# A decoder step on one Trainium2 core: two attention blocks per head as one product of whole float32 operands

## The chip, the core and the metric

The kernel runs on one core of one Trainium2 chip. A core has five engines with a queue of instructions each: TensorE (matrix products, PE in the profile, with its weight loads as PEld), VectorE (DVE), ScalarE (ACT), GpSimd (POOL) and SyncE (SP), which here issues nearly all DMAs. TensorE reads both operands from the on-chip memory SBUF and writes its results to the accumulator memory PSUM. Engines wait for each other on semaphores.

The metric is the device time of one execution in microseconds (us), as a median over several executions. The kernel before takes 1631.18 us (median of 3, 1631.09 to 1631.23).

## What is computed

One layer of a decoder with three parallel branches (convolution, stick-breaking attention, attention into a memory), for a prompt of 256 tokens and 8 sampled sequences of 4 tokens. All of it is float32. The change lies in the stick-breaking attention of the prompt: 8 heads of 128 channels, strictly causal, in blocks of 128 queries.

```python
def stick_breaking_block(q, k, v, q_pos, k_pos, b_sb):
    z = jnp.einsum('bqhd,bkhd->bhqk', q, k).astype(jnp.float32) * (HEAD_DIM ** -0.5)
    z = z + b_sb.astype(jnp.float32)[None, :, None, None]
    causal = k_pos[None, :] < q_pos[:, None]
    log_keep = jnp.where(causal, jax.nn.log_sigmoid(-z), 0.0)
    after = lax.cumsum(log_keep, axis=3, reverse=True) - log_keep
    a = jnp.where(causal, jnp.exp(jax.nn.log_sigmoid(z) + after), 0.0)
    return jnp.einsum('bhqk,bkhd->bqhd', a.astype(v.dtype), v)
```

With 256 prompt tokens there are two blocks of queries. The first sees 128 keys, the second 256. So each head has three blocks of 128 x 128 scores: queries 0 to 127 against keys 0 to 127, and queries 128 to 255 against keys 0 to 127 and 128 to 255.

## The kernel before

**Split operands.** The kernel keeps float32 accuracy with products of a reduced type, `float32r`. An operand x is split into a high part h, its cast to that type on ScalarE, and a low part l = x - h, a subtraction on VectorE. A product of two split operands is three products: h by h, h by l and l by h, added up in PSUM. The weights are treated so on the way in: each slab of 128 x 1024 weights is loaded, cast (L303) and subtracted (L314). The large products over these slabs run at L486, with 128 stationary columns and 288 moving ones (256 prompt and 32 sample tokens).

**Order.** The order of all instructions is written out by a planner in the kernel (`Order`, L75). Each piece of work is a generator that asks for an engine with an estimated time, for flags that it needs and for buffers of the pools `a`, `t`, `s`, `k4`, `pm`, `pa`, `pl` and others; the planner always takes the request that can start first, by rank among equals. What comes out is one fixed queue for each engine. The main stream on TensorE is the large products, and the small ones of the attention heads are put between them.

**The heads.** For each of 8 heads the main stream makes a key, a query and a value tile (`sb_key`, `sb_query`, `sb_head`, started from L1420 to L1423). Key and query are normalised (`head_norm`) into a float32 tile `box[0]` and split (L1067, L1075) into a pair of tiles (`Pair`, L845). The value tile is transposed in two blocks (L1103, L1104) and split (L1108). Then `sb_head` computes

1. the scores: `three` (L849) at L1117 for the second 128 queries against all 256 keys, and at L1118 for the first 128 queries against the first 128 keys, both into one PSUM tile `zp` of 384 columns;
2. the attention weights from them on ScalarE and VectorE (L1122 to L1141);
3. three transposes (L1145), and the split of the 384 columns (L1148 on ScalarE, L1150 on VectorE);
4. the value product: `three` at L1157 with the first 128 values for all 256 queries, and at L1158 with the last 128 values for the last 128 queries, added to columns 128 to 255 of the same PSUM tile.

The helper `three` issues its products at L851, L852 and L853; all uses of it in the kernel, those of the memory attention too, show these lines. The product at L1225 (`first` in `sb_sample`, once for each of two groups of four sampled heads) is made of whole float32 operands, as are those of the sampled sequences at L1012, L1026 and L1182, which have 32 stationary columns.

Of the kernel before, what the change touches and what calls it, by code (L numbers as in the profile page):

```python
# [7 lines left out]
F32 = mybir.dt.float32  # L8
F32R = mybir.dt.float32r
# [5 lines left out]
P = 128  # L15
D_MODEL = 2048
KT = D_MODEL // P
NP = 256
# [3 lines left out]
T = NP + NS  # L22
# [52 lines left out]
class Order:  # L75
# [15 lines left out]
    def add(self, gen, rank, at=None):  # L91
        job = Job(gen, rank, self.now.ready if at is None and self.now else at or 0.0)
        self.jobs.append(job)
        was, self.now = self.now, job
        self.step(job)
        self.now = was
# [10 lines left out]
    def give(self, pool, n=1):  # L107
        self.pools[pool] += [self.now.ready] * n
# [45 lines left out]
def dve(n, *flags, **take):  # L154
    return Ask("DVE", 0.18 + n / 920.0, flags, **take)


def act(n, *flags, **take):
    return Ask("ACT", 0.22 + n / 1200.0, flags, **take)
# [6 lines left out]
def pe(us, *flags, **take):  # L166
    return Ask("PE", us, flags, **take)
# [15 lines left out]
def tile_decoder_step(ctx: ExitStack, tc: tile.TileContext, xT, memT, wall, cvec, kmat, ptab,  # L183
                      kpool, vpool, mkc, mvc, hist,
                      yT, oK, oV, oCp, oCs, oMK, oMV):
    nc = tc.nc
# [16 lines left out]
    give, add, done = order.give, order.add, order.set  # L203
# [3 lines left out]
    def tl(p, shape, dt=F32):  # L207
        cnt[0] += 1
        return pools[p].tile(shape, dt, tag=p, name=f"{p}_{cnt[0]}")

    def bank(p):
        return tl(p, [P, 512])
# [43 lines left out]
    def col(c):  # L256
        return cv[:, c:c + 1]
# [388 lines left out]
    def store(dst, src):  # L646
        yield sp(late=Order.HOP + Order.SLACK["SP"])
        nc.sync.dma_start(dst, src)
# [159 lines left out]
    def head_norm(ps, gcol, box, flag, p="pm"):  # L808

        yield dve(T, rx_done, t=4)  # L810
        raw, sq, hl, r = (tl("t", [P, T], F32R if i == 2 else F32) for i in range(4))
        nc.vector.tensor_mul(raw, ps, rx)
        give(p)
        yield act(T)
        nc.scalar.activation(sq, raw, AF.Square)
        yield dve(T)
        top, low = slice(0, P // 2), slice(P // 2, P)
        nc.vector.tensor_add(sq[top], sq[top], sq[low])
        yield act(T)
        nc.scalar.copy(hl[top], sq[top])  # L820
        yield dve(T)
        nc.vector.tensor_sub(hl[low], sq[top], hl[top].bitcast(F32))
        yield pe(MM, pa=1, late=1.5)
        ss = bank("pa")[:, :T]
        nc.tensor.matmul(ss, ones_r, hl, start=True, stop=True)  # L825
        yield from rsqrt_of(ss, T, HD, sq, r, r)
        give("pa")
        yield dve(T, a=1)
        out = tl("a", [P, T])
        nc.vector.scalar_tensor_tensor(out, raw, col(gcol), r, op0=ALU.mult, op1=ALU.mult)  # L830
        give("t", 4)
        box.append(out)
        done(flag)

    def split(a, src, n, flag=None):

        yield act(n, a=2)
        a.take()
        nc.scalar.copy(a.h[:, :n], src)
        yield dve(n)  # L840
        nc.vector.tensor_sub(a.l[:, :n], src, a.h[:, :n].bitcast(F32))
        if flag is not None:
            done(flag)

    class Pair:  # L845
        def take(self):
            self.h, self.l = tl("a", [P, T], F32R), tl("a", [P, T], F32R)

    def three(out, x, y, cx, cy, first=True, last=True):  # L849

        nc.tensor.matmul(out, x.h[:, cx], y.h[:, cy], start=first, stop=False)  # L851
        nc.tensor.matmul(out, x.h[:, cx], y.l[:, cy], start=False, stop=False)  # L852
        nc.tensor.matmul(out, x.l[:, cx], y.h[:, cy], start=False, stop=last)  # L853
# [201 lines left out]
    ks, qs_ = [None] * SH, [None] * SH  # L1055
    k_made, q_made, v_made = ([Flag() for _ in range(SH)] for _ in range(3))
# [3 lines left out]
    def sb_key(h):  # L1060
        def evac(ps):
            box, ks[h] = [], Pair()
            yield from head_norm(ps, C_GK, box, Flag())
            add(store(oK[h], box[0]), 3)
            yield act(NS)
            nc.scalar.copy(kn[:, h, :], box[0][:, NP:])
            yield from split(ks[h], box[0][:, :NP], NP, k_made[h])  # L1067
            give("a")
        return evac

    def sb_query(h):
        def evac(ps):
            box, qs_[h] = [], Pair()
            yield from head_norm(ps, C_GQ, box, Flag())
            yield from split(qs_[h], box[0][:, :NP], NP, q_made[h])  # L1075
            yield act(NS)
            nc.scalar.copy(qs[:, h, :], box[0][:, NP:])
            give("a")
            done(qs_made[h])
        return evac  # L1080

# [9 lines left out]
    def sb_head(h):  # L1091
        def evac(ps):
            yield dve(T, rx_done, a=1)
            v = tl("a", [P, T])
            nc.vector.tensor_mul(v, ps, rx)
            give("pm")
            add(store(oV[h], v), 3)
            yield act(NS)
            nc.scalar.copy(vs[:, h % 4 * NS:(h % 4 + 1) * NS], v[:, NP:])
            last = h % 4 == 3  # L1100
            yield pe(0.33 if last else 0.22, pa=1)
            tp = bank("pa")[:, :3 * P]
            nc.tensor.transpose(tp[:, 0:P], v[:, 0:P], ident)  # L1103
            nc.tensor.transpose(tp[:, P:2 * P], v[:, P:2 * P], ident)  # L1104
            if last:
                nc.tensor.transpose(tp[:, 2 * P:3 * P], vs, ident)
            vt = Pair()
            yield from split(vt, tp[:, :2 * P], 2 * P)  # L1108
            if last:
                yield act(P)  # L1110
                nc.scalar.copy(vn[:, h // 4, :], tp[:, 2 * P:3 * P])
            give("pa")
            give("a")
            done(v_made[h])
            yield pe(0.54, k_made[h], q_made[h], pa=1, s=3)
            zp = bank("pa")[:, :384]
            three(zp[:, 128:384], qs_[h], ks[h], slice(P, NP), slice(0, NP))  # L1117
            three(zp[:, 0:128], qs_[h], ks[h], slice(0, P), slice(0, P))  # L1118
            give("a", 4)
            z, l, sp_ = (tl("s", [P, 512]) for _ in range(3))  # L1120
            yield act(384)
            nc.scalar.activation(z[:, :384], zp, AF.Identity, scale=SCALE, bias=col(C_BSB + h))  # L1122
            give("pa")
            zz, ll, ss = z[:, :384], l[:, :384], sp_[:, :384]
            yield from softplus_parts(zz, ll)
            yield dve(384)
            nc.vector.scalar_tensor_tensor(ss, zz, 0.0, ll, op0=ALU.max, op1=ALU.add)
            yield dve(256)
            nc.vector.tensor_mul(blocks2(sp_, P), blocks2(sp_, P), twice(caus, P))
            yield dve(384)  # L1130
            nc.vector.scalar_tensor_tensor(zz, zz, 0.0, ll, op0=ALU.min, op1=ALU.subtract)
            yield dve(2 * 384)
            nc.vector.tensor_tensor_scan(ll[:, ::-1], ones_s[:, :384][:, ::-1], ss[:, ::-1], 0.0,
                                         op0=ALU.mult, op1=ALU.add)
            yield dve(384)
            nc.vector.tensor_sub(zz[:, :383], zz[:, :383], ll[:, 1:])
            give("s")
            yield act(384)
            act_fn(LN_EXP, zz, zz, AF.Exp)
            yield dve(256)  # L1140
            nc.vector.tensor_mul(blocks2(z, P), blocks2(z, P), twice(caus, P))  # L1141
            yield pe(0.35, pa=1)
            tp = bank("pa")[:, :384]
            for i in range(3):
                nc.tensor.transpose(tp[:, i * P:(i + 1) * P], z[:, i * P:(i + 1) * P], ident)  # L1145
            yield act(384, s=2)
            hh, low = tl("s", [P, 512], F32R), tl("s", [P, 512], F32R)[:, :384]
            nc.scalar.copy(hh[:, :384], tp)  # L1148
            yield dve(384)
            nc.vector.tensor_sub(low, tp, hh[:, :384].bitcast(F32))  # L1150
            give("pa")
            give("s", 2)
            w = Pair()
            w.h, w.l = hh, low
            yield pe(0.54, pa=1)
            op = bank("pa")[:, :NP]
            three(op, vt, w, slice(0, P), slice(0, NP), last=False)  # L1157
            three(op[:, P:NP], vt, w, slice(P, 2 * P), slice(256, 384), first=False)  # L1158
            give("s", 2)
            give("a", 2)  # L1160
            yield act(NP, a=2)
            a = osb[h] = Acts()
            nc.scalar.copy(a.h[:, :NP], op)
            yield dve(NP)
            nc.vector.tensor_sub(a.l[:, :NP], op, a.h[:, :NP].bitcast(F32))
            give("pa")
            done(osb_made[h])
        return evac
# [441 lines left out]
```

## Time and profile before

| what | before |
|---|---|
| median of 3 executions | 1631.18 us |
| profiled execution, its own time | 1630.64 us |
| its span, first to last instruction | 1628.9 us |
| granted clock of TensorE, mean | 1.000 |
| memory read, written | 296.99 MB, 6.32 MB |
| main products, L486, with pool `a` and high weights | x5184, 293 ns each |

The profile is one execution. "Busy" is the time in which an engine had an instruction running; an instruction's duration is a latency, and TensorE's instructions overlap, so what one costs is read from the distance between starts. A row of the groups gives line, engine, operation, output<-inputs, shapes, count, busy time and mean duration, and after the bar the idle time before it and what ended that. PEld rows are the weight loads of TensorE, which run beside its products. A row of the timeline merges equal neighbours and gives start, duration and count.

### The profile page before, as it was taken

To read this page: it belongs to the slowest core of one execution; us is meant where nothing else is said; L and a number is where in the kernel's file an instruction comes from. 1 tells how busy PE (TensorE), PEld (TensorE's weight loads), DVE (VectorE), ACT (ScalarE), POOL (GpSimd) and SP (SyncE) were. 2 spreads that over 40 slices of the span, in tenths; PEclk is the share of its full clock that TensorE was granted. 3 is DMA by queue.
4 is the path that set the end of the run, shared out by engine and by line. 5 is a ranking of instruction groups with operands and counts; after the bars stand their busy time and mean duration, and the time that the engine had idled before them with its cause. 6 is when DMAs were issued, how large, how long until landed. Compare 5 with 4: busy or idle time off the path is not lost.

```text
span 1628.9 us, 30880 instructions
## 1 busy us (share of the span) xinstructions
PE 1624.3 (100%) x12760; PEld 1608.8 (99%) x12760; DVE 996.7 (61%) x1478; ACT 737.9 (45%) x1066; POOL 139.0 (9%) x106
## 2 busy tenths in 40 slices
PE   9999999999999999999999999999999999999999
PEld 7999999999999999999999999999999999999999
DVE  7999888877777655565555544455445554455543
ACT  8846766654433534444443333333333333333332
POOL 0020000000000000001222200121001210022100
PEclk9999999999999999999999999999999999999999
DMA  9787474667755555556655555555555555555563
GB/s 327 226 182 256 151 263 150 223 224 275 282 179 169 167 170 170 168 160 207 195 172 168 171 173 168 167 171 172 168 169 168 168 169 168 169 168 169 180 193 100
DMA packets 107103, 305.33 MB, mean 187 GB/s; under 512 B 19922, under 2 KB 29522, under 8 KB 106962
## 3 DMA queue, kind: packets, MB, share of 16 engines
q1 hardware_dynamic: 106818, 303.33, 59.1%
q8 instruction: 100, 1.64, 0.4%
q14 instruction: 41, 0.34, 0.1%
q10 hardware_dynamic: 144, 0.02, 0.0%
HBM read 296.99 MB, written 6.32 MB: 186 GB/s over the span
## 4 chain that ended last, share of the span: by engine, by line
PE 100%; POOL 0%; DVE 0%; issue 0%; POOLq 0%
PE pm L486 93%; PE pm L539 3%; PE pa L486 1%; PE pl L1012 1%; PE pl L1182 0%; PE pa L853 0%; PE pa L852 0%; PE pa L851 0%; PE pl L1026 0%; PE pa L1406 0%; PE pa L825 0%; PE pa L1145 0%; PE pa L906 0%; PE pa L1103 0%; PE pa L633 0%; PE pa L1104 0%
## 5 line engine op out<-in xcount | busy, mean ns | idle before, releaser
L303 ACT CAST wh<-wr 128x1024 fp32r<-128x1024 f32 (+1 forms) x520 | 530.3, 1023 | 628.0 <-PE pm L486 568.7
L486 PE MATMUL pm<-a,wh 128*128 128x288 f32 x5184 | 739.1, 293 | 0.0
L314 DVE TENSOR_TENSOR wl<-wr,wh 128x1024 fp32r<-128x1024 f32 (+1 forms) x520 | 620.1, 1196 | 184.4 <-ACT wh L303 183.2
L486 PEld LDWEIGHTS pm<-a,wh 128*128 128x128 f32 x5184 | 695.9, 188 | 0.4 <-issue 0.4
L486 PE MATMUL pm<-a,wl 128*128 128x288 f32 x2592 | 397.9, 292 | 0.0
L486 PEld LDWEIGHTS pm<-a,wl 128*128 128x128 f32 x2592 | 358.3, 188 | 0.4 <-issue 0.4
L486 PE MATMUL pm<-k,wh 128*128 128x288 f32 x2400 | 337.9, 292 | 0.0
L486 PEld LDWEIGHTS pm<-k,wh 128*128 128x128 f32 x2400 | 321.0, 188 | 0.0
L486 PE MATMUL pm<-k,wl 128*128 128x288 f32 x1200 | 182.0, 292 | 0.0
L486 PEld LDWEIGHTS pm<-k,wl 128*128 128x128 f32 x1200 | 165.1, 188 | 0.0
L1343 POOL TENSOR_TENSOR t<-t 128x288 f32<-128x288 f32 x64 | 96.5, 1508 | 599.7 <-DVE t L1340 599.7
L1357 DVE TENSOR_TENSOR a<-a,pm 128x288 f32<-128x288 f32 x64 | 29.1, 455 | 122.7 <-PE pm L486 122.7
L1340 DVE SCALAR_TENSOR_TENSOR t<-pm,rx 128x288 f32<-128x288 f32 x64 | 29.2, 458 | 90.5 <-PE pm L486 90.5
L1346 ACT CAST k<-t 128x288 fp32r<-128x288 f32 x60 | 25.9, 433 | 123.9 <-POOL t L1343 123.9
L1259 DVE TENSOR_TENSOR t<-pm,rx 128x288 f32<-128x288 f32 x48 | 22.0, 458 | 76.2 <-PE pm L486 76.2
L1348 DVE TENSOR_TENSOR k<-t,k 128x288 fp32r<-128x288 f32 x60 | 27.4, 458 | 59.2 <-ACT k L1346 59.2
L717 DVE SCALAR_TENSOR_TENSOR a<-a,cv,a 128x256 f32<-128x256 f32 x120 | 59.5, 496 | 1.4
L1329 POOL TENSOR_TENSOR t<-t,t 128x288 f32<-128x288 f32 x15 | 21.3, 1418 | 389.9 <-ACT t L1326 389.9
L539 PE MATMUL pm<-wh,a 128*128 128x512 f32 x128 | 34.8, 394 | 0.0
L486 PE MATMUL pm<-s,wh 128*128 128x288 f32 x160 | 33.7, 292 | 0.0
L539 PEld LDWEIGHTS pm<-wh,a 128*128 128x128 f32 x128 | 24.3, 191 | 5.7 <-ACT wh L303 0.6
L486 PEld LDWEIGHTS pm<-s,wh 128*128 128x128 f32 x160 | 25.3, 188 | 0.0
(205 smaller groups left out, 755.3 us busy)
## 6 DMA issues: line engine op xcount, KB each, us to landing
wr<-in_wall SPq DMA_DIRECT2D x488, 512.0 KB, 3.6
wr<-in_wall SPq DMA_DIRECT2D x32, 256.0 KB, 4.9
k<-in_kpool SPq DMA_DIRECT2D x32, 256.0 KB, 5.9
k<-in_vpool SPq DMA_DIRECT2D x32, 256.0 KB, 6.1
k<-in_mkc SPq DMA_DIRECT2D x8, 512.0 KB, 8.6
k<-in_mvc SPq DMA_DIRECT2D x8, 512.0 KB, 7.2
t<-in_xT SPq DMA_DIRECT2D x16, 144.0 KB, 3.7
out_yT<-a SPq DMA_DIRECT2D x16, 144.0 KB, 1.9
```

What stands on the lines that cost most here:

```text
L303: nc.scalar.copy(sl.h[:, c], sl.raw[:, c])
L314: nc.vector.tensor_sub(sl.l[:, c], sl.raw[:, c], sl.h[:, c].bitcast(F32))
L486: nc.tensor.matmul(ps, w, a, start=(first and i == 0), stop=(last and i == len(todo) - 1))
L539: nc.tensor.matmul(ps[m], y[:, m * P:(m + 1) * P], z[:, w], start=(k == 0 and j < 2), stop=(k == KT - 1 and j in (4, 5)))
L717: nc.vector.scalar_tensor_tensor(c[:, :NP], up[:, k:k + NP], w, c[:, :NP], op0=ALU.mult, op1=ALU.add)
L1259: nc.vector.tensor_mul(g, ps, rx)
L1329: nc.gpsimd.tensor_add(sq_sum[0], sq_sum[0], res[0])
L1340: nc.vector.scalar_tensor_tensor(r, ps, 0.0, r2, op0=ALU.max, op1=ALU.mult)
L1343: nc.gpsimd.tensor_mul(r, r, r)
L1346: nc.scalar.copy(a.h, r)
L1348: nc.vector.tensor_sub(a.l, r, a.h.bitcast(F32))
L1357: nc.vector.tensor_add(x1[j], x1[j], ps)
```

## The change

The block of the first 128 queries against the first 128 keys, and the block of the last 128 attention weights against the last 128 values, are each one product of whole float32 operands. The parts that only these blocks used are no longer split: of the query, only the last 128 columns; of the value, only the first 128; of the transposed attention weights, only the first 256. The last block of values and of weights is copied from PSUM as it is, on ScalarE. The key is still split whole. A new class `Half` holds both parts in one tile.

```diff
     def split(a, src, n, flag=None):
-        yield act(n, a=2)
+        yield act(n, a=a.tiles)
...
     class Pair:
+        tiles = 2
         def take(self):
             self.h, self.l = tl("a", [P, T], F32R), tl("a", [P, T], F32R)
+    class Half:
+        tiles = 1
+        def take(self):
+            x = tl("a", [P, T], F32R)
+            self.h, self.l = x[:, :P], x[:, P:2 * P]
...
             nc.scalar.copy(kn[:, h, :], box[0][:, NP:])
+            ks[h].raw = box[0]
             yield from split(ks[h], box[0][:, :NP], NP, k_made[h])
-            give("a")
...
-            box, qs_[h] = [], Pair()
+            box, qs_[h] = [], Half()
             yield from head_norm(ps, C_GQ, box, Flag())
-            yield from split(qs_[h], box[0][:, :NP], NP, q_made[h])
+            qs_[h].raw = box[0]
+            yield from split(qs_[h], box[0][:, P:NP], P, q_made[h])
             yield act(NS)
             nc.scalar.copy(qs[:, h, :], box[0][:, NP:])
-            give("a")
...
-            vt = Pair()
-            yield from split(vt, tp[:, :2 * P], 2 * P)
+            vt = Half()
+            yield from split(vt, tp[:, :P], P)
+            yield act(P, a=1)
+            vt.raw = tl("a", [P, T])[:, :P]
+            nc.scalar.copy(vt.raw, tp[:, P:2 * P])
...
-            three(zp[:, 128:384], qs_[h], ks[h], slice(P, NP), slice(0, NP))
-            three(zp[:, 0:128], qs_[h], ks[h], slice(0, P), slice(0, P))
-            give("a", 4)
+            nc.tensor.matmul(zp[:, 0:128], qs_[h].raw[:, 0:P], ks[h].raw[:, 0:P], start=True, stop=True)
+            three(zp[:, 128:384], qs_[h], ks[h], slice(0, P), slice(0, NP))
+            give("a", 5)
...
-            yield act(384, s=2)
-            hh, low = tl("s", [P, 512], F32R), tl("s", [P, 512], F32R)[:, :384]
-            nc.scalar.copy(hh[:, :384], tp)
-            yield dve(384)
-            nc.vector.tensor_sub(low, tp, hh[:, :384].bitcast(F32))
+            yield act(256, s=2)
+            w, raw = Pair(), tl("s", [P, 512])
+            w.h, w.l = (lambda x: (x[:, :256], x[:, 256:]))(tl("s", [P, 512], F32R))
+            nc.scalar.copy(w.h, tp[:, :256])
+            yield act(P)
+            nc.scalar.copy(raw[:, :P], tp[:, 256:])
+            yield dve(256)
+            nc.vector.tensor_sub(w.l, tp[:, :256], w.h.bitcast(F32))
...
             three(op, vt, w, slice(0, P), slice(0, NP), last=False)
-            three(op[:, P:NP], vt, w, slice(P, 2 * P), slice(256, 384), first=False)
+            nc.tensor.matmul(op[:, P:NP], vt.raw, raw[:, :P], start=False, stop=True)
```

More of the change, by code (lines that the diff above doesn't have):

```diff
@@ L1145, in evac @@
                 nc.tensor.transpose(tp[:, i * P:(i + 1) * P], z[:, i * P:(i + 1) * P], ident)
-            yield act(384, s=2)
-            hh, low = tl("s", [P, 512], F32R), tl("s", [P, 512], F32R)[:, :384]
-            nc.scalar.copy(hh[:, :384], tp)
-            yield dve(384)
-            nc.vector.tensor_sub(low, tp, hh[:, :384].bitcast(F32))
+            yield act(256, s=2)
[6 more added lines that the diff above has]
+            nc.vector.tensor_sub(w.l, tp[:, :256], w.h.bitcast(F32))
             give("pa")
             give("s", 2)
-            w = Pair()
-            w.h, w.l = hh, low
             yield pe(0.54, pa=1)
```

## The prediction

> **What bounds the kernel now.** I read four views in this order: the first and fourth part of the page, the list of TensorE's waits, the table of stretches for the time in which the changed heads run, and then the timeline of single instructions around the products that change. First the page.
>
> ```profile
> span 1628.9 us, 30880 instructions
> ## 1 busy us (share of the span) xinstructions
> PE 1624.3 (100%) x12760; PEld 1608.8 (99%) x12760; DVE 996.7 (61%) x1478; ACT 737.9 (45%) x1066; POOL 139.0 (9%) x106
> ```
>
> ```profile
> PE 100%; POOL 0%; DVE 0%; issue 0%; POOLq 0%
> PE pm L486 93%; PE pm L539 3%; PE pa L486 1%; PE pl L1012 1%; PE pl L1182 0%; PE pa L853 0%; PE pa L852 0%; PE pa L851 0%; PE pl L1026 0%; PE pa L1406 0%; PE pa L825 0%; PE pa L1145 0%; PE pa L906 0%; PE pa L1103 0%; PE pa L633 0%; PE pa L1104 0%
> ```
>
> TensorE works for the whole span and is the whole chain that ended last. A busy TensorE need not be one that never waits, so the list of its waits comes next. It has one row.
>
> ```profile
> PE pa L1406 <- POOL eps L233: 1.3, 1, 1.3
> ```
>
> The only wait is 1.3 us at the start (the warm-up). The changed heads run between 160 and 360 us. The table of stretches has, in order, the length, the busy time of PE, PEld (weight loads), DVE, ACT and POOL with their counts, and the granted clock.
>
> ```profile
> 160.00:250.00 90.00, 90.00 (x703) 90.00 (x703) 77.18 (x142) 61.38 (x124) 0.00 (x0) 1.00 0.61 199
> 250.00:360.00 110.00, 110.00 (x997) 107.87 (x996) 92.54 (x170) 66.86 (x126) 3.00 (x4) 1.00 0.59 195
> ```
>
> PE is full there at clock 1.00. DVE has 77.18 of 90 and 92.54 of 110 us, ACT less. So the time can only change in two ways: TensorE's queue gets shorter or longer work, or something arrives late for it. What VectorE and ScalarE save is worth nothing as long as PE does not wait.
>
> **The change on TensorE.** Per head, six products with 128 moving columns go: three after the scores (L1118) and three after the values (L1158). They run through the helper at L851 to L853, so they are found by their shape.
>
> ```profile
> L853 PE MATMUL pa<-s,a 128*128 128x128 f32 x8 | 2.2, 277 | 0.0
> L852 PE MATMUL pa<-a,a 128*128 128x128 f32 x8 | 2.2, 276 | 0.0
> L853 PE MATMUL pa<-a,a 128*128 128x128 f32 x8 | 2.2, 273 | 0.0
> ...
> L1225 PE MATMUL pl<-vn,t 128*128 128x128 f32 x4 | 0.8, 272 | 0.0
> ```
>
> x8 for the values (pa<-s,a) and x8 for the scores (pa<-a,a) is 16 places with three products each. The 277 ns are a latency with a modelled end; what TensorE loses to one product is the distance from its start to the next start. Here is the last head's place in the timeline (start, duration, engine).
>
> ```profile
> 355.47 0.22 PE L851 MATMUL pa<-s,a 128*128 128x128 f32 x1
> 355.47 0.19 PEld L852 LDWEIGHTS pa<-s,a 128*128 128x128 f32 x1
> 355.53 0.27 PE L852 MATMUL pa<-s,a 128*128 128x128 f32 x1
> 355.58 0.19 PEld L853 LDWEIGHTS pa<-s,a 128*128 128x128 f32 x1
> 355.64 0.28 PE L853 MATMUL pa<-s,a 128*128 128x128 f32 x1
> 355.69 0.57 PEld L486 LDWEIGHTS pm<-a,wh 128*128 128x128 f32 x4
> 355.75 0.74 PE L486 MATMUL pm<-a,wh 128*128 128x288 f32 x4
> ```
>
> From 355.47 to 355.75 the three take **0.28 us**. Only the first passes in 0.06 (355.47 to 355.53); the next two stand 0.11 apart, as do the weight loads (355.47, 355.58, 355.69). With only 128 columns to stream, a product is over before the next weights are loaded, so the weight load sets the pace.
>
> What comes in their place is one product of whole float32 operands, 128x128 by 128x128. The trace has this very shape: L1225 multiplies whole float32 tiles, once for each of two groups, and shows x4, so one such product is two instructions. Its surroundings:
>
> ```profile
> 379.70 1.59 PE L486 MATMUL pm<-a,wh 128*128 128x288 f32 x11
> 381.12 0.38 PE L1225 MATMUL pl<-vn,t 128*128 128x128 f32 x2
> 381.44 3.77 PE L1012 MATMUL pl<-k,k 128*32 128x128 f32 x128
> ```
>
> The 11 products of L486 before it take 1.42 us to its start, 0.129 each, their usual pace, so going over to whole operands costs nothing. The two instructions end 0.38 us after the first began and one lasts 0.272, so they stand 0.11 apart. The next start is at 381.44, 0.32 after the first: the second took 0.21. But what follows there has another shape (128*32, four products side by side in the array), and the changed places are followed by ordinary 128*128 products of split operands. For that step back the nearest row is the transposes, which also read whole float32 with 128 columns.
>
> ```profile
> 253.97 0.49 PE L1145 MATMUL pa<-km,s 128*128 128x128 f32 x3
> 254.21 0.78 PE L486 MATMUL pm<-a,wh 128*128 128x288 f32 x4
> 254.83 1.20 PE L486 MATMUL pm<-a,wl 128*128 128x288 f32 x8
> ```
>
> Three transposes and four L486 products take 0.86 us; without 4 x 0.129 = 0.52 that leaves 0.34, or 0.115 for each transpose, the step back included. So I charge the whole product 0.11 + 0.115 = **0.225 us**. The bounds are 0.22 (twice 0.11, no step at all) and 0.32 (L1225 with what follows it there). I take the transposes' end because they stand between the same kinds of products as the new one will.
>
> By the Trainium skill (TensorEngine Tiling (Array Packing), section Tiling Modes, Key Properties) a change of the array's tiling mode drains the engine. That would put the excess of L1225 down to the narrow products behind it; if it belongs to the whole product itself, the sum takes the 0.32.
>
> The sum: 16 x (0.225 - 0.28) = **-0.88 us**; by the bounds 16 x (0.22 - 0.28) = -0.96 and 16 x (0.32 - 0.28) = +0.64. The 256-column products around these places stay, and only the order within the scores changes (the whole product first). A product cheaper than 0.22 is excluded: two instructions of this shape never stand closer than 0.11 in these rows.
>
> **The change on the other engines.**
>
> ```profile
> L1148 ACT CAST s<-pa 128x384 fp32r<-128x384 f32 x8 | 3.8, 480 | 12.5 <-PE pa L1145 12.5
> ...
> L839 ACT CAST a<-pa 128x256 fp32r<-128x256 f32 x8 | 2.9, 367 | 1.4 <-PE pa L1104 0.7 <-PE pa L1106 0.7
> ...
> L1111 ACT COPY vn<-pa 128x128 f32<-128x128 f32 x2 | 0.5, 250 | 0.0
> ```
>
> ```profile
> L1150 DVE TENSOR_TENSOR s<-pa,s 128x384 fp32r<-128x384 f32 x8 | 4.4, 556 | 4.9 <-ACT s L1148 4.9
> L1165 DVE TENSOR_TENSOR a<-pa,a 128x256 fp32r<-128x256 f32 x8 | 3.4, 421 | 2.9 <-ACT a L1163 2.9
> L841 DVE TENSOR_TENSOR a<-pa,a 128x256 fp32r<-128x256 f32 x8 | 3.4, 419 | 0.2 <-ACT a L839 0.2
> ```
>
> VectorE: three subtractions per head lose 128 columns (query, value, attention weights). 556 - 419 = 137 ns each, 0.41 us a head, 3.3 us in all. ScalarE: the query's cast loses 128 columns (367 - 250 = 0.12), the value's 256 become 128 + 128 (2 x 0.25 - 0.37 = +0.13), the weights' 384 become 256 + 128 (0.37 + 0.25 - 0.48 = +0.14): +0.15 us a head, 1.2 us in all. Both hide behind PE, at nothing; without that cover ScalarE's share would be at most 1.2 us. No DMA, SyncE or GpSimd work is added. Each head holds one more buffer of pool `a` (raw key and raw query kept, the query's parts in one tile instead of two), of 75.
>
> One wait is added: the value product now also needs the raw copy of the last attention block, ScalarE's new instruction between the cast and the product. Behind that product in TensorE's queue stand the ordinary L486 products. How much room there is, the last head shows:
>
> ```profile
> 352.19 0.48 ACT L1148 CAST s<-pa 128x384 fp32r<-128x384 f32 x1 [1.88 <-PE pa L1145]
> ...
> 352.76 1.05 ACT L303 CAST wh<-wr 128x1024 fp32r<-128x1024 f32 x1
> 352.77 0.55 DVE L1150 TENSOR_TENSOR s<-pa,s 128x384 fp32r<-128x384 f32 x1
> ...
> 355.11 0.28 PE L851 MATMUL pa<-s,a 128*128 128x256 f32 x1
> ```
>
> The last operand is ready at 352.77 + 0.55 = 353.32 and the product starts at 355.11, 1.79 us later. Cast and copy end at 352.19 + 0.37 + 0.25 = 352.81, or at 353.86 with one weight cast of 1.05 between them. I cost the wait at nothing.
>
> **Rivals.**
> (a) *Streaming counts, not the weight loads.* Each of L1225's two instructions takes 0.11, twice the 0.06 in which a split product streams its 128 columns (355.47 to 355.53). If the columns streamed were what TensorE pays for, with the loads hidden, a place would go from three such streams to four: 16 x 0.06 = +0.96 us, 1632.1. Against it: the three products took 0.28 and not 3 x 0.06. The Trainium skill (FP8 and Floating Point Precision, TensorE Precision Notes) has the rule behind it: true FP32 goes through the array in four passes. L1225's 2 x 0.11 agrees with that count, but the trace does not agree that three split products cost only three.
> (b) *The step back is paid at each place.* 0.32 instead of 0.225: +0.64 us, 1631.8. For it: L1225 itself shows 0.32. Against it: the transposes.
> (c) *Slower: TensorE stands before the value product.* Place: the raw copy waits on ScalarE behind weight casts (1.05 each). Three casts would end the copy at 352.81 + 3.15 = 355.96, 0.85 after the start of 355.11; eight heads make 6.8 - 0.88 = +5.9 us, 1637.1. It decides from the third cast on. Against it: the rows above have one cast in that stretch, and ACT is busy 61.38 of 90 us.
> (d) *The compiler makes more than two instructions of the product.* With four at 0.11 a place costs 0.44: 16 x 0.16 = +2.6 us, 1633.8. L1225 speaks against it.
> (e) *VectorE's relief shortens the time*, by up to its 3.3 us: 1631.18 - 0.88 - 3.3 = 1627.0. That needs a PE that waits for it, and the list of waits has none after the start.
>
> **How the numbers follow.** The profiled execution took 1630.64 us (span 1628.9 and 1.74 around it); with -0.88 it is 1629.8 and its span 1628.0. It lies 0.54 below the median of 1631.18, from which I predict 1631.18 - 0.88 = **1630.3 us**. 0.2% is 3.3 us, about what a measurement of this kernel can tell from no change, so the forecast counts as no change. Chances: forecast 0.66, (a) 0.11, (b) 0.11, (c) 0.06, (d) 0.04, (e) 0.02. Faster by over 0.2% is (e), 0.02; slower is (c), 0.06; all else, 0.92, is within. The range reaches from the forecast's bound of 1631.18 - 0.96 = 1630.2 to (a)'s 1632.1, and on both sides 0.5 further, the distance between the two times of the kernel before: 1629.7 to 1632.6. It leaves out (c), (d) and (e), 0.12.
>
> **What would show it.** In the changed profile, the rows of L851 to L853 with 128x128 must be gone, and two lines of the head must show float32 products, x16 each, near 272 ns. TensorE's instructions should be 12760 - 48 + 32 = 12744, give or take lost records. In the timeline the whole product's two starts stand 0.11 apart and the next start 0.115 behind the second; 0.21 there means (b). The list of TensorE's waits stays empty after the start; a wait on ScalarE before the value product means (c). The forecast is wrong if a place costs over 0.28 us, or if PE idles between 160 and 360 us.

## The result, and the profile after

| | before | changed kernel |
|---|---|---|
| median | 1631.22 us (22 runs) | 1629.32 us (22 runs) |
| profiled execution, span | 1628.9 us | 1627.2 us |
| TensorE instructions | 12760 | 12744 |

The ratio is 0.9988, with a 95% interval from 0.9983 to 0.9994. The kernel became 1.9 us faster, 0.12%. The forecast was 0.88 us and the range ended at 1629.7: the sign and the place were right, the size was less than half of what came, and the time lies 0.4 us under the range. All medians leave out three executions that took far longer (1938 to 5761 us).

The head of the page and the whole list of TensorE's waits in the changed kernel read:

```profile
span 1627.2 us, 30882 instructions
## 1 busy us (share of the span) xinstructions
PE 1622.6 (100%) x12744; PEld 1606.7 (99%) x12744; DVE 994.0 (61%) x1478; ACT 736.9 (45%) x1082; POOL 139.0 (9%) x106
```

```profile
PE pa L1419 <- POOL eps L233: 1.3, 1, 1.3
```

TensorE has 16 instructions fewer, as forecast (48 go, 32 come), and still waits for nothing after the warm-up (L1419 is L1406 of before). The two new products, by group (line, engine, output<-inputs, shape, count, busy us, mean ns):

```profile
L1171 PE MATMUL pa<-s,a 128*128 128x128 f32 x16 | 3.1, 274 | 0.0
L1129 PE MATMUL pa<-a,a 128*128 128x128 f32 x16 | 3.1, 274 | 0.0
```

x16 for eight heads: two instructions for each whole product, with the 0.27 us of L1225. Nothing is left of the 128x128 rows of the helper (now L860 to L862). The stretch of the heads, with the columns as in the prediction's table:

```profile
160.00:250.00 90.00, 90.00 (x703) 90.00 (x703) 77.70 (x147) 61.52 (x133) 0.00 (x0) 1.00 0.63 205
250.00:360.00 110.00, 110.00 (x1095) 107.59 (x1094) 91.02 (x179) 65.75 (x136) 4.01 (x5) 1.00 0.68 226
```

The second stretch counts more instructions than before because two blocks of 128 narrow sample products (L1021) now fall into it instead of one. PE is as full as before and at the same clock, so all of the gain must be less work on TensorE. This is a value place in the timeline after:

```profile
183.56 0.28 PE L860 MATMUL pa<-s,a 128*128 128x256 f32 x1
183.67 0.28 PE L861 MATMUL pa<-s,a 128*128 128x256 f32 x1
183.79 0.29 PE L862 MATMUL pa<-s,a 128*128 128x256 f32 x1
183.91 0.39 PE L1171 MATMUL pa<-s,a 128*128 128x128 f32 x2
184.05 0.77 PE L486 MATMUL pm<-a,wh 128*128 128x288 f32 x4
184.66 0.43 PE L486 MATMUL pm<-a,wl 128*128 128x288 f32 x2
```

To compare it with the place that the prediction showed (355.11 to 355.75 before), one more row of before is needed, the one behind its four L486 products:

```profile
356.34 1.20 PE L486 MATMUL pm<-a,wl 128*128 128x288 f32 x8
```

Both stretches hold three products over 256 columns, the block, and four L486 products. Before it is 356.34 - 355.11 = 1.23 us, after 184.66 - 183.56 = 1.10: 0.13 less, not the forecast's 0.055. Taken at full resolution from the starts of all places that stand alone between L486 products (6 score and 7 value places before, 6 and 5 after; from the last L486 start ahead to the third behind, less three steps of 0.130), a score place costs 0.698 us before and 0.586 after, a value place 0.701 and 0.589. That is **0.112 us a place**, and 16 x 0.112 = 1.79 of the 1.9 us.

A score place after, where the whole product comes first:

```profile
259.97 0.38 PE L1129 MATMUL pa<-a,a 128*128 128x128 f32 x2
260.10 0.36 PE L860 MATMUL pa<-a,a 128*128 128x256 f32 x1
260.31 0.28 PE L861 MATMUL pa<-a,a 128*128 128x256 f32 x1
260.42 0.28 PE L862 MATMUL pa<-a,a 128*128 128x256 f32 x1
260.54 2.24 PE L486 MATMUL pm<-a,wh 128*128 128x288 f32 x16
```

The product behind the whole one seems to start 0.13 or 0.14 after its first instruction, 0.02 to 0.03 after the second, where the prediction looked for 0.115; then comes a long step, 260.10 to 260.31. A start in this trace can run ahead of what TensorE has done, and the next step makes up for it. So the price of a place is only right when both ends of the window lie among even steps.

### The profile page after: what moved, and what is told of

It reads as the page before. It is cut to its first block, busy times and chain, and to the rows that moved or that the text cites. A ratio compares the mean times of both kernels' runs of the same rounds, so it can differ in the third digit from the quotient of the medians.

```text
span 1627.2 us, 30882 instructions
## 1 busy us (share of the span) xinstructions
PE 1622.6 (100%) x12744; PEld 1606.7 (99%) x12744; DVE 994.0 (61%) x1478; ACT 736.9 (45%) x1082; POOL 139.0 (9%) x106
## 4 chain that ended last, share of the span: by engine, by line
PE 100%; POOL 0%; DVE 0%; issue 0%; POOLq 0%
PE pm L486 93%; PE pm L539 3%; PE pa L486 1%; PE pl L1021 1%; PE pl L1195 0%; PE pa L860 0%; PE pa L862 0%; PE pa L861 0%; PE pl L1035 0%; PE pa L1419 0%; PE pa L1157 0%; PE pa L825 0%; PE pa L915 0%; PE pa L1171 0%; PE pa L1129 0%; PE pa L1112 0%
## 5 line engine op out<-in xcount | busy, mean ns | idle before, releaser
L486 PE MATMUL pm<-a,wh 128*128 128x288 f32 x5184 | 737.1, 293 | 0.0
L486 PEld LDWEIGHTS pm<-a,wh 128*128 128x128 f32 x5184 | 696.2, 188 | 0.0
L486 PE MATMUL pm<-a,wl 128*128 128x288 f32 x2592 | 399.2, 293 | 0.0
L486 PEld LDWEIGHTS pm<-a,wl 128*128 128x128 f32 x2592 | 359.0, 188 | 0.6 <-issue 0.6
L486 PE MATMUL pm<-k,wh 128*128 128x288 f32 x2400 | 337.8, 292 | 0.0
L486 PEld LDWEIGHTS pm<-k,wh 128*128 128x128 f32 x2400 | 321.5, 188 | 0.0
L486 PE MATMUL pm<-k,wl 128*128 128x288 f32 x1200 | 181.8, 292 | 0.0
L486 PEld LDWEIGHTS pm<-k,wl 128*128 128x128 f32 x1200 | 165.5, 188 | 0.0
L539 PE MATMUL pm<-wh,a 128*128 128x512 f32 x128 | 35.0, 395 | 0.0
L486 PE MATMUL pm<-s,wh 128*128 128x288 f32 x160 | 33.7, 292 | 0.0
L539 PEld LDWEIGHTS pm<-wh,a 128*128 128x128 f32 x128 | 24.2, 190 | 5.9 <-ACT wh L303 1.0
L486 PEld LDWEIGHTS pm<-s,wh 128*128 128x128 f32 x160 | 25.6, 188 | 0.0
```

The source lines that it names most:

```text
L486: nc.tensor.matmul(ps, w, a, start=(first and i == 0), stop=(last and i == len(todo) - 1))
L539: nc.tensor.matmul(ps[m], y[:, m * P:(m + 1) * P], z[:, w], start=(k == 0 and j < 2), stop=(k == KT - 1 and j in (4, 5)))
```

## The experiments

Two theories for the 1.9 us. **Loads**: TensorE gave up three weight loads of 0.112 us at a place (0.336, where the prediction read 0.28) and pays 0.226 for the whole product; nothing else counts. **Relief**: TensorE saves only the forecast 0.055 at a place, and the other microsecond comes from the shorter work of VectorE and ScalarE. Differences in us are against the kernel before in the same session: 1631.12 for the score block alone, the kernel with all parts split and the two fivefold ones, 1631.36 for the last row, 1631.10 for the others.

| kernel | median us | difference | ratio, 95% interval |
|---|---|---|---|
| score block alone whole | 1630.13 | -0.99 | 0.9997, 0.9987 to 1.0006 |
| value block alone whole | 1629.97 | -1.13 | 0.9993, 0.9985 to 1.0002 |
| both whole, all parts still split | 1629.18 | -1.94 | 0.9989, 0.9980 to 0.9998 |
| before, split score block five times | 1641.91 | +10.79 | 1.0067, 1.0053 to 1.0080 |
| changed, whole score block five times | 1636.51 | +5.39 | 1.0035, 1.0021 to 1.0048 |
| changed, all scores whole | 1629.88 | -1.22 | 0.9992, 0.9983 to 1.0000 |
| before, split score block 256 wide | 1631.21 | +0.11 | 1.0001, 0.9992 to 1.0010 |
| changed, whole product last | 1629.22 | -1.88 | 0.9988, 0.9979 to 0.9997 |
| before, four extra triples with 64 stationary | 1637.40 | +6.04 | 1.0038, 1.0024 to 1.0051 |

**Both blocks whole, everything split as before.** The relief is taken away and the products stay.

```diff
-            box, qs_[h] = [], Half()
+            box, qs_[h] = [], Pair()
...
-            vt = Half()
-            yield from split(vt, tp[:, :P], P)
+            vt = Pair()
+            yield from split(vt, tp[:, :2 * P], 2 * P)
...
+            w.h, w.l = tl("s", [P, 512], F32R), tl("s", [P, 512], F32R)
+            nc.scalar.copy(w.h[:, :384], tp)
...
+            nc.vector.tensor_sub(w.l[:, :384], tp, w.h[:, :384].bitcast(F32))
```

> Both blocks are whole products as in the changed kernel, but query, value and attention weights are split whole as before (the parts that are not used are made and dropped), so VectorE and ScalarE are not relieved; ScalarE has two more copies per head than before. 'Loads': TensorE's work is that of the changed kernel, 1.8 us faster than before, within 0.3 us of the changed kernel. 'Relief': only the 0.9 us of TensorE are left, 1630.3.

It takes 1629.18 us, as the changed kernel does. Its page:

```profile
PE 1622.6 (100%) x12744; PEld 1606.6 (99%) x12744; DVE 997.6 (61%) x1478; ACT 744.3 (46%) x1084; POOL 138.2 (8%) x106
```

VectorE is 3.6 us busier than in the changed kernel (994.0) and ScalarE 7.4 us (736.9), and the time does not show it. TensorE has the same 12744 instructions. The list of TensorE's waits in this kernel has one row more than that of the changed one:

```profile
PE pm L539 <- ACT wh L303: 0.6, 1, 0.6
```

This wait lies in the first 20 us of the profiled execution (1629.6 us), long before the heads. The profiles of the value block alone, of all scores whole, of the whole product last and of the 64 stationary columns have one too, of 0.3 to 0.8 us; what brings it on is not shown. It does not touch the comparison: from the last start of L539 to TensorE's last start this kernel takes 1574.7 us, the changed one 1574.4 and the kernel before 1576.4. The relief is worth nothing that can be measured, so **relief falls**.

**The price of each form, fivefold.** To measure the disputed price by itself, the score block is issued five times, split in the kernel before and whole in the changed one.

```diff
-            three(zp[:, 0:128], qs_[h], ks[h], slice(0, P), slice(0, P))
+            for _ in range(5):
+                three(zp[:, 0:128], qs_[h], ks[h], slice(0, P), slice(0, P))
```

> The kernel before, with the three split products of the score block issued five times instead of once (each time from a fresh start, same result): 32 more triples. 'Loads': 32 x 0.336 = +10.8 us over before, and the starts in the row of 15 products stand 0.11 apart. The reading on record, 0.28 a triple: +9.0 us, with one 0.06 step in each triple.

32 extra triples cost 10.79 us, **0.337 each**, as "loads" said to 0.1 us. Some of the 15 products of one place:

```profile
220.07 0.28 PE L853 MATMUL pa<-a,a 128*128 128x256 f32 x1
220.18 0.22 PE L851 MATMUL pa<-a,a 128*128 128x128 f32 x1
220.24 0.28 PE L852 MATMUL pa<-a,a 128*128 128x128 f32 x1
220.35 0.27 PE L853 MATMUL pa<-a,a 128*128 128x128 f32 x1
220.46 0.28 PE L851 MATMUL pa<-a,a 128*128 128x128 f32 x1
220.57 0.28 PE L852 MATMUL pa<-a,a 128*128 128x128 f32 x1
...
221.69 0.27 PE L853 MATMUL pa<-a,a 128*128 128x128 f32 x1
221.81 1.00 PE L486 MATMUL pm<-a,wl 128*128 128x288 f32 x6
```

The step of 0.06 (220.18 to 220.24) comes once, at the edge from 256 to 128 columns. All others are 0.11, those from one triple to the next too (220.35 to 220.46). It is no saving of the first product: it is where the starts run ahead, and the place gives it back behind its last product: the six L486 products there take 1.00 us, where six even ones take 0.29 + 5 x 0.13 = 0.94.

```diff
-            nc.tensor.matmul(zp[:, 0:128], qs_[h].raw[:, 0:P], ks[h].raw[:, 0:P], start=True, stop=True)
+            for _ in range(5):
+                nc.tensor.matmul(zp[:, 0:128], qs_[h].raw[:, 0:P], ks[h].raw[:, 0:P], start=True, stop=True)
```

> The changed kernel, with the whole product of the score block issued five times instead of once: 32 more. Both theories charge two instructions of 0.11: 32 x 0.22 = +7.0 us over the changed kernel, +5.1 over before. Were the product paid with a step of its own each time (0.32), +10.2 over the changed kernel.

It is 5.39 us over before, and the changed kernel is 1.90 under it, so 32 extra whole products cost 7.29 us, **0.228 each**, where 0.22 was expected and the prediction had 0.225. 0.337 - 0.228 = 0.109 a place, 1.7 us for sixteen. The places of the two kernels give 0.334 and 0.223, a difference of 0.111.

**What sets the 0.112.** First the columns streamed are doubled, with the loads as they are; the second half of the result is not used.

```diff
+            wide = bass.AP(tensor=zb.tensor, offset=zb.offset, ap=[list(zb.ap[0]), [384, 2], [1, P]])
...
-            three(zp[:, 0:128], qs_[h], ks[h], slice(0, P), slice(0, P))
+            three(wide, qs_[h], ks[h], slice(0, P), slice(0, NP))
```

> The kernel before, with the three split products of the score block over 256 moving columns instead of 128 (the second half of the result is not used). 'Loads': the load paces 128 columns already, so 3 x 0.118 instead of 3 x 0.112: 8 x 0.02 = +0.15 us over before. The reading on record, 0.28 for three: 8 x (0.354 - 0.28) = +0.6 us.

+0.11 us, with an interval on both sides of zero, which alone would not part 0.15 from 0.6 safely. The places do: the six score places that stand alone cost 0.721 on average, against 0.698 before, so the three products cost 0.022 more and not 0.07. Twice the columns are nearly free. Then the loads are halved and the columns kept, in four extra triples per head whose result is overwritten.

```diff
+            for _ in range(4):
+                three(zp[0:64, 0:128], qs_[h], ks[h], slice(0, 64), slice(0, P))
             three(zp[:, 0:128], qs_[h], ks[h], slice(0, P), slice(0, P))
```

> The kernel before, with four extra triples of split products per head ahead of the score block's own, each over 128 moving columns but with only 64 stationary ones (half a weight load; the result is overwritten by the block's own triple): 32 extra triples, as many as in the fivefold split block, which cost 10.8 us. 'Loads': a product's price is its weight load, so half a load is some 0.056 us and about what 128 columns take to stream: 32 x 3 x 0.06 = 5.8 us, plus 16 changes between array shapes of about 0.09 each, 1.5 us: +7.3 over before. Rival 'floor': 0.11 us is what any product costs, whatever it loads: 10.8 + 1.5 = +12.3 us.

96 extra products cost 6.04 us, 0.063 each. The timeline, with the edges into and out of the narrow products:

```profile
219.36 0.28 PE L853 MATMUL pa<-a,a 128*128 128x256 f32 x1
219.48 0.22 PE L851 MATMUL pa<-a,a 128*64 128x128 f32 x1
219.53 0.22 PE L852 MATMUL pa<-a,a 128*64 128x128 f32 x1
...
220.13 0.23 PE L853 MATMUL pa<-a,a 128*64 128x128 f32 x1
220.20 0.27 PE L851 MATMUL pa<-a,a 128*128 128x128 f32 x1
220.31 0.27 PE L852 MATMUL pa<-a,a 128*128 128x128 f32 x1
220.42 0.27 PE L853 MATMUL pa<-a,a 128*128 128x128 f32 x1
```

From 219.48 to 220.20 twelve products take 0.72, 0.06 each; as soon as 128 columns are loaded again, the steps are 0.11. A fixed floor of 0.11 per product is refuted: the price of a split product with few moving columns goes with the width of its weights. The 1.5 us expected for the changes of shape did not come: 6.04 - 96 x 0.060 leaves 0.28 us for 16 changes, under 0.02 each.

**One block alone.** Each half of the change, with the other half as before.

```diff
-            nc.tensor.matmul(op[:, P:NP], vt.raw, raw[:, :P], start=False, stop=True)
+            three(op[:, P:NP], vt, w, slice(P, 2 * P), slice(256, 384), first=False)
```

> Only the score block is one whole product; the value block and all its splits are as before. Theory 'loads': what TensorE gives up at a place is three weight loads of 0.112 us, not the 0.28 us read between starts, and it pays 0.226 for the whole product, so a place is worth 0.11 us: 8 x 0.11 = 0.9 us faster than before (about 1630.3). Rival 'relief': TensorE saves 0.055 at a place, and the rest of the change's 1.9 us comes from VectorE, which has three shorter subtractions per head; with one of the three that is 0.44 + 0.34 = 0.8 us. The time alone does not part the two; the place in the timeline does: 0.59 us for the score place under 'loads', 0.64 under 'relief'.

```diff
-            nc.tensor.matmul(zp[:, 0:128], qs_[h].raw[:, 0:P], ks[h].raw[:, 0:P], start=True, stop=True)
-            three(zp[:, 128:384], qs_[h], ks[h], slice(0, P), slice(0, NP))
+            three(zp[:, 128:384], qs_[h], ks[h], slice(P, NP), slice(0, NP))
+            three(zp[:, 0:128], qs_[h], ks[h], slice(0, P), slice(0, P))
```

> Only the value block is one whole product; the score block, key and query are as before. 'Loads': 8 x 0.11 = 0.9 us faster than before, the value place at 0.59 us and the score place at 0.70. 'Relief': VectorE keeps two of its three shorter subtractions, 0.44 + 0.67 = 1.1 us faster.

-0.99 and -1.13 us, each with an interval that includes no change, so the times alone settle nothing; they add up to -2.12 against -1.90 of both. The places do: with the scores alone, a score place costs 0.588 and a value place stays at 0.699; with the values alone 0.699 and 0.587. The two halves are worth the same and do not depend on each other.

**How far it carries.** All scores as whole products; key and query are not split at all.

```diff
-            yield from split(ks[h], box[0][:, :NP], NP, k_made[h])
+            done(k_made[h])
...
-            yield from split(qs_[h], box[0][:, P:NP], P, q_made[h])
+            done(q_made[h])
...
-            three(zp[:, 128:384], qs_[h], ks[h], slice(0, P), slice(0, NP))
+            nc.tensor.matmul(zp[:, 128:384], qs_[h].raw[:, P:NP], ks[h].raw[:, 0:NP], start=True, stop=True)
```

> The changed kernel, but the scores of the second 128 queries are one whole product too (256 moving columns), so key and query are not split at all. 'Loads': a split product over 256 columns streams for 0.118 us, longer than its weight load, and three are 0.36; the whole one streams twice 256 at half pace, 0.43: 8 x 0.07 = 0.6 us slower than the changed kernel. 'Relief': VectorE loses another 8 x (0.42 + 0.28) = 5.6 us of subtractions, so the kernel is faster than the changed one.

-1.22 against the changed kernel's -1.90: 0.68 us slower than that by the medians. The intervals of the two ratios overlap, so the place has to decide: a score place costs 0.661 instead of 0.586, 8 x 0.075 = 0.6. With 256 moving columns the split form wins again, although VectorE is freed of more work. This too speaks against relief, and it puts the crossing between 128 and 256 columns. The group and one place of the product over 256 columns:

```profile
L1130 PE MATMUL pa<-a,a 128*128 128x256 f32 x16 | 4.8, 380 | 0.0
```

```profile
214.65 0.60 PE L1130 MATMUL pa<-a,a 128*128 128x256 f32 x2
214.90 1.14 PE L486 MATMUL pm<-a,wh 128*128 128x288 f32 x6
```

Its two instructions stand 0.60 - 0.38 = 0.22 apart, where those over 128 columns stand 0.11 apart, with weights of the same width. So the price of a whole product goes with its columns, already from 128 to 256, where the price of a split one hardly moves.

**The order in the place.** The whole product behind the split ones.

```diff
-            nc.tensor.matmul(zp[:, 0:128], qs_[h].raw[:, 0:P], ks[h].raw[:, 0:P], start=True, stop=True)
             three(zp[:, 128:384], qs_[h], ks[h], slice(0, P), slice(0, NP))
+            nc.tensor.matmul(zp[:, 0:128], qs_[h].raw[:, 0:P], ks[h].raw[:, 0:P], start=True, stop=True)
```

> The changed kernel, with the whole product of the scores behind the three split ones instead of ahead of them. 'Loads': same sum of work, within 0.2 us of the changed kernel. A price that hangs on what follows a whole product (256 or 288 columns) would show as a difference of up to 8 x 0.1 = 0.8 us.

1629.22 us, 0.02 from the changed kernel by the differences, and 0.585 instead of 0.586 at the place. What follows a whole product does not matter, as long as it has the same array shape.

## Why the prediction was half right

*What bounds the kernel: right.* TensorE never waits in the stretch of the heads; with 3.6 us more on VectorE and 7.4 on ScalarE the time is the same.

*The whole product's price: right.* 0.225 was charged, 0.228 measured by repetition, in two instructions 0.11 apart. Taking the transposes and not the surroundings of L1225 was right. The changed kernel has one place where the narrow products of the sampled sequences follow one of the new whole products:

```profile
250.86 0.38 PE L1171 MATMUL pa<-s,a 128*128 128x128 f32 x2
251.18 3.77 PE L1021 MATMUL pl<-k,k 128*32 128x128 f32 x128
```

Here it is 0.32 to the next start, as with L1225; elsewhere it is not. The excess belongs to the step to products with 32 stationary columns, so rival (b) fell. The Trainium skill (TensorEngine Tiling (Array Packing), Tiling Modes) puts a drain at such a change, and these rows agree that such a change costs time (0.32 against 0.228). The step to 64 stationary columns (219.36 to 219.48) shows none; whether it is a change of mode, no row tells.

*The removed products' price: wrong. This is the step that failed:* "From 355.47 to 355.75 the three take 0.28 us. Only the first passes in 0.06". They take 0.337, with which the sum would have been 16 x (0.225 - 0.337) = -1.79 us. The window ended at the first L486 start, which had run ahead by 0.06, and the row behind it shows the debt: four L486 products in 0.74 us at 355.75, where four even ones take 0.29 + 3 x 0.13 = 0.68. For the transposes the prediction had closed its window one row later and got the right price; for the removed products it had not. It bounded only the price of what comes and took the price of what goes for a plain reading, so the range did not hold the error: 16 x 0.057 = 0.9 us, nearly all of the miss.

*The other engines: right in what matters, nearly right in size.* VectorE's busy time fell by 2.7 us where 3.3 was taken. ScalarE's fell by 1.0 where 1.2 more was taken, although the durations of its changed rows add up to 1.7 more: busy time counts overlapping instructions once. The new copies in the changed kernel:

```profile
L1163 ACT COPY s<-pa 128x128 f32<-128x128 f32 x8 | 2.2, 272 | 0.0
L1120 ACT COPY a<-pa 128x128 f32<-128x128 f32 x8 | 2.1, 265 | 0.1
```

0.27 us each where 0.25 was taken. The added wait on the raw copy (rival (c)) never showed: the list of waits is empty after the start.

*The other rivals.* (a), paying by columns streamed, fell for the split products with the block that costs nearly the same over twice the columns. For the whole product it holds from 128 to 256 columns (0.11 and 0.22 for an instruction). The Trainium skill (FP8 and Floating Point Precision, TensorE Precision Notes) counts four passes for true FP32. The trace agrees at 256 columns, where the two instructions take 0.44 and one split product 0.12. At 128 columns the whole product still wins, because each of the three split products costs 0.112, nearly twice the 0.060 that it costs over the same columns with 64 stationary ones. (d) fell with the x16 rows, (e) with the kernel that splits everything.

*The chances.* "Within 0.2%" had 0.92, and 0.12% is within it; the interval of the ratio (0.9983 to 0.9994) does not reach 1 all the same, so 22 runs tell more than the 0.2% assumed.

## What to carry to other kernels

Where few columns move, a split product on TensorE costs its weight load and not its stream: 0.112 us with 128 stationary columns, over 128 moving columns and hardly more over 256. A whole float32 product costs two instructions that grow with the columns, 0.11 each over 128 and 0.22 over 256. As far as these runs go, price each instruction by the larger of its load and its stream. At 128 x 128 two float32 instructions (0.228) beat three split products (0.337); at 256 moving columns the three win.

Price what is removed with the same care as what is added: extend the window until the steps are even on both sides, or repeat the piece and divide, and give the removed side bounds of its own.

## What was not expected of the hardware

The recorded start of a product can run ahead where the pace changes (0.05 to 0.06 us from a 256-column product to a 128-column one, 0.08 behind a whole product or a transpose, 0.19 behind a whole one over 256 columns: 0.03 in place of 0.22), and one later step is longer by about as much. Why it does so, no run shows. A change between 128 and 64 stationary columns costs nothing that the starts show and under 0.02 us by the time, while one to 32 costs about 0.09 us (0.32 against 0.228 at a whole product).
